# Moving eight first products of a lookup pass into the ranking stage, and six instead of two pairs behind the last expert weight

## The chip, the cores and the metric

The kernel runs on one core of a Trainium2 chip. The metric is the device time of one execution in microseconds (us). The core's engines are named as in the profile: PE multiplies matrices (PEld loads its weights), DVE works on vectors, ACT evaluates functions and also issues some DMAs, POOL is GpSimd, SP issues most DMAs.

## The reference

The program computes two blocks on 256 tokens of width 1024. The first is a token mixer with banded attention and a mixture of 32 experts (top 4). The second has two layers with a latent stream and a context stream of 256 tokens each. Each stream of a layer goes through a mixer and then through a large table lookup:

```python
def peer_ffn(h, w_q, sub_keys, u_tab, v_tab):
    # per block xb of 128 tokens
    q = (xb @ w_q).reshape(128, 8, 2, 64)
    s = einsum('thpd,pkd->thpk', q, sub_keys)       # 8 heads, 2 halves, 128 sub-keys
    s1, i1 = top_k(s[:, :, 0], 16); s2, i2 = top_k(s[:, :, 1], 16)
    cand_s = s1[..., :, None] + s2[..., None, :]    # 256 candidates
    cand_i = i1[..., :, None] * 128 + i2[..., None, :]
    top_s, pos = top_k(cand_s, 16)
    idx = take_along_axis(cand_i, pos); wts = softmax(top_s)
    act = gelu(einsum('thkd,td->thk', u_tab[idx], xb)) * wts
    return einsum('thk,thkd->td', act, v_tab[idx])  # tables of 16384 rows of 1024
```

The context stream goes through the first layer's lookup only. It depends on nothing of the first block, so its work can be done beside the experts.

## The kernel before

All 16384 rows of both tables are read and multiplied for all tokens (`peer_pass`, L838), in 64 pairs of 2 x 128 rows. The first product of a pair (`u_stage`, L861) is rows of `p_u` times the tokens; its gelu is the tile `ge`. `a_stage` (L898) multiplies it by a grid that is zero where a token did not choose a row and holds its weight where it did. The second product (`v_stage`, L921, `v_part` L908) multiplies the result by rows of `p_v` and adds it up in four PSUM banks of tag `a`. The product of a pair is done one pair after its first one.

Products of this kind are in three parts: `wload` (L141) loads 128x1024 weights (512 KB) into `wr`, ACT copies them rounded into `wh` (L147), DVE subtracts to get the rest `wl` (L148), and PE multiplies three times (L157 to L159 for the first product, L914, L915 and L917 for the second). `wr`, `wh` and `wl` have three buffers each.

`peer_prep` (L816) stands before a pass: queries (`p_w_q`), then `topk` (L719) for each of two blocks of 128 tokens, then `grid` (L787), which builds the selection grid and writes it to `gd` in DRAM. `topk` ranks on DVE; its last step takes the chosen table rows out of the candidates with one fused instruction for each head and place (L768), 128 for a block. `peer_pass` can do first products ahead of the pass (`ahead`): `early` pairs, whose `ge` is either kept or written to DRAM (`sdr`) and read back by `prefetch` (L886) some pairs ahead of its use. The two latent passes do 40 pairs so; the context pass none.

`moe` (L970) runs the experts two at a time: `expert_load` (L549) brings 24 weights of 1 MiB for such an expert pair into four buffers, all on SP's queue; gate and up products are L1096, the down product L1130, the scatter L1142 and its addition on DVE L1143. `overflow` (L1146) is a conditional block after the first two expert pairs.

The order of each engine's instructions is fixed ahead of time by a scheduler that goes by priorities and its own estimate of durations. Work inside `with filler()` has the lowest priority. There are two such stretches: the first holds the context mixer and the first eight steps (`PB`) of the context `peer_prep`; the second (L1267) holds the rest of it, and the context pass. Between them `overflow` and the remaining experts are written (`drain(mgen)`, L1266), with which the second stretch runs side by side. After them comes the latent branch (`chunk_mlp` with `a_w_v`, `a_w_u`, `a_w_out`, then its own `peer_prep` and pass).

`fetch` (L853) is the load of a pass. Where `late` is given, the loads of the last `late[0]` pairs are put behind the last expert weight in SP's order (`queued`):

```python
if late is not None and at_pair[0] >= npair - late[0]:
    queued(ins, late[1])
```

PSUM has eight banks: two of tag `g` (experts, latent products), two of `u`, four of `a`. In the kernel before, the context ranking takes `u` banks, the grid `a` banks and the context first products `u` banks.

## Time and profile before

| | us |
|---|---|
| median of 3 runs | 4162.1 |
| lowest, highest | 4159.7, 4166.0 |
| the profiled execution | 4160.3 |
| its span in the trace | 4158.5 |
| PE busy | 4020.3 (97%) |
| DVE busy | 2381.3 (57%) |
| ACT busy | 1929.3 (46%) |
| POOL busy | 169.7 (4%) |
| DMA | 1115 MB, mean 268 GB/s |

The span is what the trace shows; the time of the execution has 1.8 us more around it. Busy shares are means over stages that are limited by different things, so a stage is read by itself: which engine is full, what the granted clock of PE is (1.00 is 2.4 GHz, 0.50 is 1.2 GHz), and how much of DMA's time is used. Matmuls are pipelined: the mean duration of one is longer than the distance between two, and the distance is what it costs.

### The profile page before, as it was taken

The page shows a single profiled execution, that of the slowest core. Times are in us where ns is not written, and L with a number is a line of the kernel's source. Part 1 is how long each engine was busy: PE and PEld are TensorE (multiplying, and loading weights), DVE is VectorE, ACT ScalarE, POOL GpSimd, SP SyncE. Part 2 cuts the span into 40 slices and gives each one's busy share as a digit, 9 for nine tenths or more (in the row PEclk, how much of TensorE's full clock was granted, in tenths as well). Part 3 has the DMA queues.
Part 4 walks back from the last instruction along what each step waited for, and adds up shares of the span by engine and source line. Part 5 has one row for each costly group of instructions (what it writes and reads, how often), then busy time and mean ns, then how long its engine had stood idle before and what let it go on. Part 6 is the DMA issues. An engine that isn't in the chain of part 4 may idle for free.

```text
span 4158.5 us, 63267 instructions
## 1 busy us (share of the span) xinstructions
PE 4020.3 (97%) x23842; PEld 3070.1 (74%) x23842; DVE 2381.3 (57%) x6357; ACT 1929.3 (46%) x2836; POOL 169.7 (4%) x230
## 2 busy tenths in 40 slices
PE   8999979999999999999999999999998899999998
PEld 7676535566666666666588998788787699988887
DVE  4464696533333333333378996565455789766555
ACT  5543245433333333333243885345545349744443
POOL 0000001100000000000000120000000002200000
PEclk9999989999999999999999999999998899999999
DMA  7659879998889898998865679766774246787773
GB/s 255 243 189 360 326 285 345 363 337 321 340 325 341 318 344 310 352 344 323 314 198 171 211 257 327 255 227 220 259 255 146 97 153 232 261 289 242 236 236 126
DMA packets 340046, 1115.49 MB, mean 268 GB/s; under 512 B 28934, under 2 KB 128006, under 8 KB 283672
## 3 DMA queue, kind: packets, MB, share of 16 engines
q1 hardware_dynamic: 323896, 1043.22, 70.2%
q10 hardware_dynamic: 15552, 66.07, 4.0%
q8 instruction: 190, 3.11, 0.3%
q0 software_dynamic: 288, 2.10, 0.1%
q14 instruction: 120, 0.98, 0.1%
HBM read 1041.97 MB, written 69.30 MB: 267 GB/s over the span
## 4 chain that ended last, share of the span: by engine, by line
PE 74%; DVE 6%; DMA 4%; ACT 2%; issue 1%; SPq 0%; POOL 0%; ACTq 0%; DVEq 0%; POOLq 0%
PE ps_g L1096 9%; PE ps_a L915 8%; PE ps_a L914 8%; PE ps_a L917 8%; PE ps_u L157 8%; PE ps_u L158 8%; PE ps_u L159 8%; PE ps_g L1130 4%; PE ps_a L811 3%; PE ps_g L1142 1%; DVE wl L148 1%; DVE eq L768 1%; DMA mo<-in_w_up_dram 1%; DMA mo<-in_w_gate_dram 1%; PE ps_g L210 1%; PE ps_g L351 1%
## 5 line engine op out<-in xcount | busy, mean ns | idle before, releaser
L148 DVE TENSOR_TENSOR wl<-wr,wh 128x1024 fp32r<-128x1024 f32 x933 | 1131.8, 1221 | 1038.7 <-ACT wh L147 1031.7
L147 ACT ACTIVATE wh<-wr 128x1024 fp32r<-128x1024 f32 x933 | 979.5, 1055 | 1268.6 <-PE ps_u L158 523.4
L915 PE MATMUL ps_a<-wl,ah 128*128 128x512 f32 x1536 | 587.2, 398 | 3.3 <-DVE wl L148 3.1
L914 PE MATMUL ps_a<-wh,ah 128*128 128x512 f32 x1536 | 571.8, 397 | 1.1 <-ACT ah L117 1.1
L1096 PE MATMUL ps_g<-mo,xg 128*64 128x512 f32 x2048 | 471.5, 603 | 11.7 <-DMA mo<-in_w_up_dram 9.3
L917 PE MATMUL ps_a<-wh,al 128*128 128x512 f32 x1536 | 478.3, 396 | 0.2 <-DVE al L118 0.2
L914 PEld LDWEIGHTS ps_a<-wh,ah 128*128 128x128 f32 x1536 | 287.9, 188 | 80.3 <-issue 12.5
L915 PEld LDWEIGHTS ps_a<-wl,ah 128*128 128x128 f32 x1536 | 286.2, 188 | 76.8 <-issue 13.3
L917 PEld LDWEIGHTS ps_a<-wh,al 128*128 128x128 f32 x1536 | 286.7, 188 | 71.8 <-issue 6.1
L1096 PEld LDWEIGHTS ps_g<-mo,xg 128*64 128x64 f32 x2048 | 137.6, 137 | 264.4 <-issue 236.3
L157 PE MATMUL ps_u<-xbh,wh 128*128 128x256 f32 x1088 | 313.3, 288 | 0.0
L158 PE MATMUL ps_u<-xbl,wh 128*128 128x256 f32 x1088 | 312.7, 288 | 0.0
L159 PE MATMUL ps_u<-xbh,wl 128*128 128x256 f32 x1088 | 312.6, 287 | 0.0
L157 PE MATMUL ps_u<-xah,wh 128*128 128x256 f32 x960 | 275.9, 288 | 2.7 <-ACT sp L881 2.7
L159 PE MATMUL ps_u<-xch,wl 128*128 128x256 f32 x960 | 274.1, 287 | 4.4 <-DVE wl L148 4.4
L159 PE MATMUL ps_u<-xah,wl 128*128 128x256 f32 x960 | 273.8, 287 | 3.2 <-DVE wl L148 3.2
L158 PE MATMUL ps_u<-xal,wh 128*128 128x256 f32 x960 | 275.5, 287 | 0.0
L157 PE MATMUL ps_u<-xch,wh 128*128 128x256 f32 x960 | 274.5, 286 | 0.2 <-ACT wh L147 0.2
L158 PE MATMUL ps_u<-xcl,wh 128*128 128x256 f32 x960 | 274.5, 286 | 0.0
L810 DVE TENSOR_SCALAR o<-cst,it 128x128 f32<-128x128 f32 x768 | 231.9, 345 | 36.6 <-PE ps_a L811 36.1
L1130 PE MATMUL ps_g<-mo,hT 128*64 128x512 f32 x1024 | 238.9, 609 | 7.9 <-DMA mo<-in_w_down_dram 5.1
L811 PE MATMUL ps_a<-o,o 128*128 128x128 f32 x1536 | 227.3, 278 | 12.3 <-ACT o L806 9.3
(654 smaller groups left out, 7020.3 us busy)
## 6 DMA issues: line engine op xcount, KB each, us to landing
wr<-in_p_u_dram SPq DMA_DIRECT2D x384, 512.0 KB, 5.0
wr<-in_p_v_dram SPq DMA_DIRECT2D x384, 512.0 KB, 4.9
mo<-in_w_gate_dram SPq DMA_DIRECT2D x128, 1024.0 KB, 7.7
mo<-in_w_up_dram SPq DMA_DIRECT2D x128, 1024.0 KB, 6.9
mo<-in_w_down_dram SPq DMA_DIRECT2D x128, 1024.0 KB, 7.5
gd<-stg ACTq DMA_DIRECT2D x48, 1024.0 KB, 7.0
gr<-gd SPq DMA_DIRECT2D x96, 512.0 KB, 8.5
mw<-in_w_mod_dram SPq DMA_DIRECT2D x48, 512.0 KB, 4.3
```

The source lines that it names most:

```text
L147: nc.scalar.activation(wh[:, :n], wr[:, :n], AF.Copy)
L148: low = nc.vector.tensor_sub(wl[:, :n], wr[:, :n], wh[:, :n].bitcast(F32))
L157: nc.tensor.matmul(o, wh, xh, start=first, stop=False)
L158: nc.tensor.matmul(o, wh, xl, start=False, stop=False)
L159: nc.tensor.matmul(o, wl, xh, start=False, stop=last)
L810: nc.vector.tensor_scalar(o1, iota, it[:, 0, t:t + 1], it[:, 2, t:t + 1], op0=ALU.is_equal, op1=ALU.mult)
L811: nc.tensor.matmul(bank[:, 2 * i2 + i, :], o2q[:, i, :], o1, start=True, stop=True)
L914: nc.tensor.matmul(acc[tb][hf], ah[:, ts], wh[:, hs], start=first, stop=False)
L915: nc.tensor.matmul(acc[tb][hf], ah[:, ts], wl[:, hs], start=False, stop=False)
L917: last_mm[0] = nc.tensor.matmul(acc[tb][hf], al[:, ts], wh[:, hf * 512:(hf + 1) * 512], start=False, stop=fin).ins
L1096: nc.tensor.matmul(bank[64 * i:64 * i + 64, :], xg[:, kq * 4 + k, o:o + CAP], wt[i][:, k, :], start=(kq == 0 and k == 0), stop=False, skip ...
L1130: nc.tensor.matmul(bank[64 * i:64 * i + 64, :], hT[:, kq * 4 + k, 64 * i:64 * i + 64], wt[i][:, k, :], start=(kq == 0 and k == 0), stop=(k ...
```

## The change

- `peer_prep` of the context ranks in `a` banks instead of `u` banks (`"a"`), and its grid has four buffers of `o1` instead of six.
- The context pass is created before the conditional block. While `peer_prep` goes on, `bsteps` takes one early pair after every second step, eight in all (`N_AHEAD_B`): four are written ahead of the conditional block. Their first product is computed, gelu is applied, and the 128x512 result goes to DRAM through one buffer (`sp`). Their subtraction (L148) is done by GpSimd instead of DVE. In the pass, these results are read back into the two `ge` buffers (`pf=0`: in the pair's own step).
- The loads of the last six pairs (before: two) stand behind the last expert weight.
- In `topk`, for all three rankings, the fused instructions are replaced: for each of 16 places one comparison, one multiplication and one sum over 128x400, on one buffer.

```diff
--- before.py
+++ after.py
@@ -36,7 +36,8 @@
 QS = 4
 GB = 4
 GG = ('g','u','a','a')
-B_LATE = 2
+B_LATE = 6
+N_AHEAD_B = 8
 MT = "u"
 M1, M2, M3 = (2,4,8)
 MI = 14
@@ -138,15 +139,15 @@
     def load(dst, src):
         last_load[0] = nc.sync.dma_start(dst, src).ins
 
-    def wload(src, n=1024, get=load, s=None):
+    def wload(src, n=1024, get=load, s=None, eng=None):
         wr = wraw(s)
         get(wr[:, :n], src)
         pl, nb = s or (st, WB)
         wh = pl.tile([P, 1024], F32R, tag="wh", name="wh", bufs=nb[1])
         wl = pl.tile([P, 1024], F32R, tag="wl", name="wl", bufs=nb[1])
         nc.scalar.activation(wh[:, :n], wr[:, :n], AF.Copy)
-        low = nc.vector.tensor_sub(wl[:, :n], wr[:, :n], wh[:, :n].bitcast(F32))
-        if hold[1]:
+        low = (eng or nc.vector).tensor_sub(wl[:, :n], wr[:, :n], wh[:, :n].bitcast(F32))
+        if hold[1] and eng is None:
             queued(low, hold[0])
             hold[1] -= 1
         return wh, wl
@@ -762,12 +763,13 @@
             nc.vector.tensor_copy(tf, tx)
             ef = tk.tile([P, 8, 16], F32, tag="ef", name="ef")
             eqs = tk.tile([P, 8, 64], F32, tag="sc", name="eq", bufs=2)
-            for h in range(8):
-                for k in range(16):
-                    eq = eqs[:, k % 8, 0:NCAND]
-                    nc.vector.scalar_tensor_tensor(eq, iota[:, 0:NCAND], tf[:, h, k:k + 1], ce[:, h, :], op0=ALU.is_equal,
-                                                   op1=ALU.mult, accum_out=ef[:, h, k:k + 1])
-                if h % 2:
+            eq = eqs[:, :, 0:NCAND]
+            for k in range(16):
+                nc.vector.tensor_tensor(eq, iota[:, None, 0:NCAND].to_broadcast([P, 8, NCAND]), tf[:, :, k:k + 1].to_broadcast([P, 8, NCAND]),
+                                        op=ALU.is_equal)
+                nc.vector.tensor_mul(eq, eq, ce)
+                nc.vector.tensor_reduce(ef[:, :, k:k + 1], eq, axis=AX.X, op=ALU.add)
+                if k % 4 == 3:
                     yield
             ei = tk.tile([P, P], I32, tag="ts", name="ei")
             e2 = tk.tile([P, P], I32, tag="tx", name="e2")
@@ -835,7 +837,7 @@
         drain(first)
         yield from grid(tk, idx[1], gd[1], bufs, 2)
 
-    def peer_pass(l, xm, pp, gd, consume, ahead=None, after=None, late=None, mark=None, npair=64, wide_end=False):
+    def peer_pass(l, xm, pp, gd, consume, ahead=None, after=None, late=None, mark=None, npair=64, wide_end=False, sub_eng=None, pf=PF):
         xh, xl = v3(xm[0]), v3(xm[1])
         acc = []
         n_keep, n_nat, n_ahead, lead, span, ra, rs, xf = ahead or (0, 0, 0, 0, 1, None, None, None)
@@ -854,7 +856,7 @@
             ins = nc.sync.dma_start(dst, src)
             queued(ins, after[0] if after else None)
             if late is not None and at_pair[0] >= npair - late[0]:
-                queued(ins, late[1])
+                queued(ins, late[1]["last"])
             if mark is not None:
                 mark[:] = [ins.ins]
 
@@ -867,7 +869,7 @@
                     for k in range(KD):
                         nc.tensor.matmul(bank[:, c * T:(c + 1) * T], wr[:, k * P:(k + 1) * P], v3(xf)[:, k, :], start=(k == 0), stop=(k == KD - 1))
                 else:
-                    wh, wl = wload(a["p_u"][l, 2 * pr + c], get=load if pr in rank else fetch)
+                    wh, wl = wload(a["p_u"][l, 2 * pr + c], get=load if pr in rank else fetch, eng=sub_eng if pr in rank else None)
                     for k in range(KD):
                         s = slice(k * P, (k + 1) * P)
                         mm3(bank[:, c * T:(c + 1) * T], (wh[:, s], wl[:, s]), (xh[:, k, :], xl[:, k, :]), k == 0, k == KD - 1)
@@ -945,11 +947,13 @@
             if rank[pr] < n_keep:
                 kept[pr] = ge
             yield "ahead"
+        for p in range(pf):
+            prefetch(p)
         grid_fetch(0)
         prev = None
         for pr in range(npair):
             at_pair[0] = pr
-            prefetch(pr + PF)
+            prefetch(pr + pf)
             if pr % 4 == GP:
                 grid_fetch(pr // 4 + 1)
             ge = kept.pop(pr) if pr in rank else u_stage(pr, False)
@@ -963,6 +967,14 @@
             for hf in range(2):
                 consume(tb, hf, acc[tb][hf])
         yield npair
+
+    class Lent:
+        def __init__(self, pl, **bufs):
+            self.pl, self.bufs, self.alias = pl, bufs, {}
+
+        def tile(self, shape, dt, tag, name, bufs):
+            tag = self.alias.get(tag, tag)
+            return self.pl.tile(shape, dt, tag=tag, name=name, bufs=self.bufs.get(tag, bufs))
 
     gds = [[dr.tile([P, 8, P, 16], F32, name=f"gd{i}{b}") for b in range(2)] for i in range(3)]
 
@@ -1259,7 +1271,19 @@
         cx_stack.close()
         tkb_stack = ctx.enter_context(ExitStack())
         tkb = pool("tkb", stack=tkb_stack, side="right")
-        bprep = peer_prep(0, XB, tkb, gds[0], (2, NB1, 3), "u")
+        bpp, bsp = Lent(None), Lent(tkb, sp=1)
+        bpass = peer_pass(0, XB, bpp, gds[0], late_res(bres, cdr, 0, 1, 5, bpp, "gr"), late=(B_LATE, mres), mark=bmark,
+                          ahead=(0, 0, N_AHEAD_B, N_AHEAD_B, 1, None, bsp, None), sub_eng=nc.gpsimd, pf=0)
+        left = [N_AHEAD_B]
+
+        def bsteps():
+            for i, _ in enumerate(peer_prep(0, XB, tkb, gds[0], (2, 4, 3), "a")):
+                if i % 2 and left[0]:
+                    drain(bpass, 1)
+                    left[0] -= 1
+                yield
+
+        bprep = bsteps()
         drain(bprep, PB)
     overflow(mo, mres)
     general("g")
@@ -1267,10 +1291,12 @@
     with filler():
         general("u", "a")
         drain(bprep)
+        drain(bpass, left[0])
         tkb_stack.close()
         pp_stack = ctx.enter_context(ExitStack())
         pp = pool("pp", stack=pp_stack, side="right")
-        bpass = peer_pass(0, XB, pp, gds[0], late_res(bres, cdr, 0, 1, 5, pp, "gr"), late=(B_LATE, mres["last"]), mark=bmark)
+        bpp.pl = bsp.pl = pp
+        bsp.bufs, bsp.alias = {"ge": 2}, {"sp": "ge"}
         drain(bpass)
         general("g")
     acc = mres["acc"]
```

## Rows read from the trace of the kernel before

**Rows 1.** busy table by stage: PE, PEld, DVE, ACT, POOL (instructions), PEclk, DMA share, GB/s

```profile
...
500.00:650.00 150.00, 121.52 (x571) 58.31 (x570) 138.63 (x1037) 65.96 (x146) 14.05 (x22) 0.89 0.73 282
650.00:787.00 137.00, 128.43 (x766) 78.35 (x766) 77.19 (x263) 83.96 (x166) 30.50 (x42) 1.00 0.93 355
787.00:936.00 149.00, 147.01 (x795) 93.94 (x792) 55.43 (x71) 50.77 (x61) 0.00 (x0) 1.00 0.93 347
936.00:1872.00 936.00, 935.50 (x5099) 606.42 (x5098) 353.69 (x446) 326.10 (x390) 0.00 (x0) 1.00 0.89 333
...
2024.00:2090.00 66.00, 60.46 (x297) 33.17 (x296) 21.37 (x31) 17.31 (x22) 0.57 (x1) 0.97 0.73 279
...
2111.00:2220.00 109.00, 97.87 (x566) 85.67 (x566) 82.95 (x111) 43.68 (x53) 8.77 (x7) 0.92 0.59 193
2220.00:2520.00 300.00, 292.93 (x2367) 286.75 (x2366) 270.44 (x1346) 214.95 (x380) 48.51 (x64) 1.00 0.65 223
```

**Rows 2.** chain of waits: start, length in us, engine, tile, line, instructions

```profile
...
2043.61 3.58 PE ps_g L1096 x16
...
2088.10 0.47 PE ps_a L917 x2
...
2275.37 0.24 PE ps_u L159 x2
```

**Rows 3.** groups by line, PE, 936 to 1872 (busy, mean ns; idle before)

```profile
...
L1096 PE MATMUL ps_g<-mo,xg 128*64 128x512 f32 x1024 | 233.4, 598 | 0.5 <-DMA mo<-in_w_gate_dram 0.4
L157 PE MATMUL ps_u<-xbh,wh 128*128 128x256 f32 x720 | 207.6, 288 | 0.0
...
L915 PE MATMUL ps_a<-wl,ah 128*128 128x512 f32 x359 | 142.4, 402 | 0.0
...
L1130 PE MATMUL ps_g<-mo,hT 128*64 128x512 f32 x528 | 120.6, 598 | 0.0
```

**Rows 4.** groups by line, PE, 495 to 640

```profile
...
L1096 PE MATMUL ps_g<-mo,xg 128*64 128x512 f32 x150 | 37.4, 642 | 6.3 <-DMA mo<-in_w_up_dram 5.5 <-DMA mo<-in_w_gate_dram 0.8
...
L1142 PE MATMUL ps_g<-yo,pt 128*128 128x512 f32 x16 | 10.6, 760 | 7.9 <-DVE xst L1143 7.5 <-ACT pt L1138 0.5
```

**Rows 5.** timeline of SP's DMA issues, 300 to 700: start, length, line, load, count

```profile
...
470.18 0.33 SPq L854 DMA_DIRECT2D wr<-in_p_u_dram  x1
...
498.88 7.31 SPq L551 DMA_DIRECT2D mo<-in_w_down_dram  x4
533.14 2.76 SPq L551 DMA_DIRECT2D mo<-in_w_gate_dram  x4
...
619.43 6.37 SPq L551 DMA_DIRECT2D mo<-in_w_gate_dram  x4
```

**Rows 6.** groups by line, PE, 640 to 690

```profile
...
L157 PE MATMUL ps_u<-xbh,wh 128*128 128x256 f32 x32 | 9.4, 295 | 0.0
```

**Rows 7.** groups by line, DVE, 520 to 832

```profile
...
L148 DVE TENSOR_TENSOR wl<-wr,wh 128x1024 fp32r<-128x1024 f32 x11 | 13.4, 1223 | 21.1 <-ACT wh L147 21.0
...
L1108 DVE TENSOR_TENSOR gt<-gt,sg 128x512 f32<-128x512 f32 x6 | 4.1, 686 | 1.4 <-ACT sg L1105 1.4
```

**Rows 8.** one line, L800 on POOL: ns min/median/max, first and last start

```profile
...
L800 POOL TENSOR_SCALAR o<-cst,it x192: 595/660/2247, 559.7 to 3621.0; 128x128 f32<-128x128 f32 x192
```

**Rows 9.** chain of waits, 600 to 640

```profile
...
618.86 3.50 DVE eq L768 x36
```

**Rows 10.** timeline of SP's DMA issues, 1990 to 2300

```profile
...
2024.20 0.33 SPq L854 DMA_DIRECT2D wr<-in_p_v_dram  x1
...
2047.22 18.47 SPq L551 DMA_DIRECT2D mo<-in_w_down_dram  x8
...
2084.60 10.87 SPq L854 DMA_DIRECT2D wr<-in_p_v_dram  x4
2098.11 6.91 SPq L139 DMA_DIRECT2D wr<-in_a_w_v_dram  x3
```

**Rows 11.** busy table of 10 us, columns as in Rows 1

```profile
...
2050.00:2060.00 10.00, 8.86 (x41) 3.02 (x39) 1.39 (x2) 0.60 (x1) 0.00 (x0) 1.00 0.87 347
```

## The prediction

> **What bounds the kernel now.** I read the busy table by stage first. Times are us from the start of the span. In the long mixed stage, 936 to 1872, where expert weights and context lookup pairs run side by side, PE is busy 935.5 of 936 us at full clock, while the DMA share is 0.89 [rows 1]. A busy PE need not be a full one, so I looked at the chain's pieces: first-product matmuls follow each other every 0.12 us, second-product ones every 0.235 us, and sixteen expert matmuls take 3.58 us [rows 2]. The counts of that stage [rows 3] at those prices fill it: 2160 first-product matmuls (45 pairs; L157 is one of three equal lines) cost 259 us, 1077 second-product ones 253 us, and the expert matmuls of eight expert pairs (1024 and 528) 348 us; the small expert work (gathers, transposes, scatters) is the rest. So that stage is PE-bound. One context pair costs 48 x 0.12 = 5.8 us for its first product and 24 x 0.235 = 5.6 us for its second, 11.4 in all. An expert pair costs about 52 us of PE; with 5.6 context pairs it takes 117 us.
>
> The stage ahead of it is another case. From 500 to 650, while the context keys are ranked, PE is idle 28.5 of 150 us at a mean granted clock of 0.89 of the 2.4 GHz level, the DMA share is 0.73 and DVE is busy 138.6 us [rows 1]. PE waits there for expert weights and for DVE's additions, which stand in DVE's queue among ranking instructions [rows 4]; no first product runs there. The DMA queue has nothing to issue between the last loads at 498.88 to 506 and 533.14, where the conditional block ends [rows 5]. From 650 to 787 (selection grids) PE is idle 8.6 us at a DMA share of 0.93.
>
> From this follows how I count. Ahead of the latent branch (about 2100) the order of work is fixed and PE's work is nearly the same before and after. The time changes by what PE's unused time changes.
>
> **The first products that come early.** Eight pairs are 8 x 5.8 = 46 us of PE work, and 16 loads of 512 KB. In the kernel before, the weights of the first pairs are already loaded from 470.18 to 496 (four p_u, two p_v, the first of them in [rows 5]) and then sit in the buffers: the two pairs' matmuls run only at 640 to 690 [rows 6], when the ranking has given up the u banks. The change gives the ranking the a banks and so frees the u banks. Net new ahead of the pass are six pairs, 34.6 us. Room: 28.5 us idle in 500 to 650 and 8.6 us in 650 to 787, 37 together; the lost clock of the first stretch ((1 - 0.89) x 121.5 = 13 us) may come back in part. DMA: 8 MiB of p_u less the 3 MiB already early, plus 2 MiB of spilled results, is 7.3 MB; at 347/0.93 = 373 GB/s that is 20 us, against 0.27 x 150 = 40 us free. SP is moved past too: these loads stand among the expert loads and each waits for one of three buffers, with expert loads queued behind it. The ends are 0 (every block delays the experts by its length) and 37 + 13 = 50, of which at most 46 can be used; I take **24 us gained**, two thirds of the idle time, because a 5.8 us block put into gaps of 2 us displaces expert work that partly meets a DMA wait later.
>
> GpSimd's subtraction of 128x1024 is not in the trace. Nearest rows: the same operation on DVE, 1.22 us [rows 7], and a 128x128 GpSimd instruction, at least 0.595 us, times eight, 4.8 us [rows 8]. Sixteen cost 20 to 77 us in a stretch of 170, two of them beside 5.8 us of PE work for each pair; I count them as hidden, and at the upper end the pairs come at 9.6 us each, 77 us, which still fits. If nothing hid them, the early products would wait for them and the gain of 24 would be lost. The Trainium skill ("GPSIMD Engine Reference", Elementwise — side-by-side cycle accounting) measures 4497 ns for a two-input add of 2048; half, 2.25 us, would be an estimate from that page, 36 us for sixteen, and the sum would be the same.
>
> **The ranking's gather.** 128 fused instructions plus accumulator reads become 48 over 128x400. Now a pair takes 3.50/18 = 0.194 us [rows 9], 24.9 us per token block. A 128x512 two-input operation takes 0.686 and a 128x1024 one 1.223 [rows 7], so 400 elements give 0.686 - 112 x 0.00105 = 0.57 us; 48 in dependence are 27.4 us. If other instructions overlap their ends by some 0.09 us, 23 us. Six blocks change by -2 to +2.5 us each. In the latent rankings PE stays covered by early first products (292.9 of 300 us busy from 2220 to 2520, DVE 270.4 [rows 1]): **0**, ends -8 and +10 for both. In the context ranking DVE is the pace: about 5 us there, and some 8 us of blocking by GpSimd; at 19% unused PE that is **2 us lost**. The o1 buffers fall from six to four; the grid stage is DMA-heavy (0.93), so I count nothing, up to 5 us.
>
> **The first eight pairs of the pass** now bring 5.6 us of PE work per 1.5 MiB (p_v, grid, spilled result) instead of 11.4 per 2.25 MiB. Expert weights bring 52/24 = 2.2 us per MiB, a v-only pair 3.7, DMA takes 2.8. Mixed as now (a third context bytes) that is 2.7 against 2.8: DMA-bound by a little over some 33 MiB. The stage 787 to 936 already stands at 0.93 [rows 1]. **3 us lost**, ends 0 and 10.
>
> **The late pairs.** Six pairs behind the last expert weight mean 26 loads there instead of 10 (p_v runs one pair behind). Context work that must finish alongside the experts falls by 34.6 + 4 x 11.4 = 80 us. In the mixed stage context work takes 65 of 117 us, so its loads run out 80/0.55 = 145 us earlier; now they run out at 2024 with about 13 MiB of expert weights to issue [rows 10]. That leaves 13 + 1.24 x 24 = 43 MiB, less some 2 that the longer stretch before has taken: 41 MiB, 1.7 expert pairs. DMA: 43 MB/373 = 115 us. PE: 1.7 x 52 = 88 us plus the lag of context work that is loaded but not multiplied (now PE is full until its first idle after 2050, 26 us after 2024 [rows 11]): 114. So they balance, and waits break it: the present tail, 2024 to 2090, has 5.5 us idle [rows 1]; I take 12.5, **7 us lost**. Ends: -3, and +26 if experts alone go as slowly as at 533 to 619, 86 us per expert pair [rows 5]. The 26 late loads keep PE busy some 74 us and cover the latent chain's normalization and transposes as ten do now.
>
> **Sum:** -24 + 2 + 0 + 3 + 7 = -12 us. The profiled run took 4160.3 us (span 4158.5, 1.8 around it), 1.8 below the median 4162.1: 4148 for that run, **4150 us** for a median.
>
> **Rivals.**
> *Late pairs fill the latent gaps.* From 2111 to 2220 PE is idle 11 us at a clock of 0.92 [rows 1], 19 us of capacity. Four more pairs could fill 15: 4135. Against it: a_w_v loads need only a buffer, yet the first is issued at 2098.11, after the last late p_v of 2084.60 to 2095 [rows 10]; buffers of one kind seem given in program order, so late pairs finish ahead of the latent weights.
> *Slower: experts alone at the end.* With context work gone, PE meets only the experts' own chain (weights, activation, transposes, down product). At 86 us per expert pair the term is +26 instead of +7: 4169. It decides from 82 us on (1.7 x 82 - 114 - 5.5 = 19, what the other terms give). For it: the only stretch with experts alone shows 86. Against it: DVE was full of ranking there, and is idle at the end.
> *Two-input instructions block each other.* The trace has one sign: GpSimd's L800 takes 0.66 us at the median and once 2.247 [rows 8], while DVE runs many two-input operations. If a GpSimd subtraction holds DVE's two-input gather for its whole length, 16 of 1.2 to 4.8 us (20 to 77 us, geometric middle 39) lengthen a DVE-bound stretch that leaves 19% of PE unused: 7 us, 4157. The Trainium skill states such a rule ("SBUF — State Buffer", Who interferes with whom): the two engines share a port pair as an exclusive lock, taken by a DVE instruction with two SBUF inputs against a GpSimd one that reads SBUF, and the later fully blocks. L800's long case agrees with it; the mean of L148, 1.223 us, shows nothing of it, but no long GpSimd operation runs there.
> *It doesn't do what it says.* The static order sets most early products behind the ranking, into 650 to 787 with 8.6 us idle: a gain of 6 instead of 24, 4168.
>
> **How the numbers follow.** Chances: forecast 0.42, latent gaps 0.13, experts alone 0.20, blocking 0.15, not early 0.10. A measurement of this kernel can tell about 0.2%, 8.3 us, from no change. Faster: 0.36 of the forecast, all of the gaps, 0.03 of blocking: 0.52. Slower: 0.14 of experts alone, 0.04 of not early, 0.03 of blocking: 0.21. Within: 0.27. The range: early gain 24 (10 to 40), tail +7 (-3 to +26) and the latent gaps give 4130 to 4173.
>
> **What would show it.** First products (L157, xb) between 490 and 650, with PE idle there falling from 28 to about 10 us and the conditional block no later than some 533 to 540; the pass starting 5 to 15 us later than 793; the last expert weight issued some 65 to 85 us earlier than 2065 with DMA at about 0.95 ahead of it; 26 p_u and p_v loads behind it; the first a_w_v load about 10 us earlier than 2098. Wrong would be: the ranking stretch longer by over 20 us, expert pairs alone above 80 us with PE idle over 20 us in the tail, or first products that still begin near 640. An a_w_v load earlier than the last late p_v would speak for filled gaps.

## The result and the profile after

The change made the kernel slower: 4212.3 us (median; 4208.9 to 4217.4) against 4160.9 for the kernel before, ratio 1.0123 [1.0111, 1.0136], about +51 us. The prediction was 4150 us within 4130 to 4173, so sign and range were both wrong. Lines stand lower in the kernel after, by one near its start and by twelve past `peer_pass`: L148 is L149, L157 is L158, the grid's product L811 is L813, and the expert products L1096 and L1130 are L1108 and L1142.

The busy table of the kernel after, by stage (PE, PEld, DVE, ACT, POOL with instructions, granted PE clock, DMA share, GB/s), to be held against [rows 1]:

```profile
...
500.00:650.00 150.00, 131.84 (x798) 85.20 (x796) 133.26 (x568) 72.24 (x126) 40.58 (x27) 0.94 0.77 287
650.00:787.00 137.00, 118.47 (x628) 64.16 (x625) 78.62 (x240) 77.31 (x168) 24.46 (x37) 0.98 0.89 322
787.00:936.00 149.00, 137.40 (x645) 77.52 (x645) 63.17 (x152) 50.74 (x76) 9.37 (x15) 0.98 0.96 358
936.00:1872.00 936.00, 936.00 (x5109) 606.70 (x5107) 356.17 (x448) 328.78 (x394) 0.00 (x0) 1.00 0.88 333
1872.00:2000.00 128.00, 121.55 (x618) 68.98 (x614) 35.02 (x46) 32.55 (x44) 0.00 (x0) 0.99 0.82 309
2000.00:2080.00 80.00, 57.69 (x230) 19.76 (x229) 10.95 (x14) 7.10 (x10) 0.00 (x0) 0.89 0.81 311
2080.00:2144.00 64.00, 64.00 (x410) 57.05 (x409) 45.89 (x64) 33.89 (x41) 2.07 (x2) 1.00 0.65 214
```

The stretches from 1872 to 2080 of the kernel before:

```profile
...
1872.00:2000.00 128.00, 128.00 (x702) 83.07 (x702) 46.20 (x56) 45.70 (x57) 0.00 (x0) 1.00 0.83 312
2000.00:2080.00 80.00, 74.46 (x368) 40.07 (x365) 22.83 (x29) 22.49 (x27) 0.00 (x0) 0.98 0.83 328
```

Part of the idle time that was to be filled is filled: from 500 to 650 PE idles 18.2 us instead of 28.5 (about 10 was expected). But it idles 18.5 instead of 8.6 in the grid stage, 11.6 instead of 2.0 from 787 to 936, and 28.8 instead of 5.5 from 1872 to 2080. SP's issues in the kernel after say the same:

```profile
...
519.18 25.79 SPq L140 DMA_DIRECT2D wr<-in_p_u_dram  x5
550.84 2.83 SPq L552 DMA_DIRECT2D mo<-in_w_gate_dram  x4
553.72 12.33 SPq L140 DMA_DIRECT2D wr<-in_p_u_dram  x3
...
847.00 0.63 SPq L856 DMA_DIRECT2D gr<-gd  x1
...
1933.99 0.33 SPq L856 DMA_DIRECT2D wr<-in_p_v_dram  x1
...
1967.80 17.61 SPq L552 DMA_DIRECT2D mo<-in_w_down_dram  x8
...
2042.89 24.23 SPq L552 DMA_DIRECT2D mo<-in_w_down_dram  x8
...
2132.42 8.92 SPq L856 DMA_DIRECT2D wr<-in_p_v_dram  x4
2143.76 15.19 SPq L140 DMA_DIRECT2D wr<-in_a_w_v_dram  x6
```

The conditional block ends at 550.8 (533.1 in [rows 5]); the pass starts with its first grid load at 847.0 (793.5 before); context loads run out at 1934 and two blocks of down-weights follow, 75 us apart, the last of them issued by 2067, no earlier than before; the first latent weight comes at 2143.8 instead of 2098.1 [rows 10]. From there to the end both kernels take the same: 2063 and 2060 us. So 46 us, nearly all of the difference, arise ahead of the latent branch.

### The profile page after: what moved, and what is told of

Same layout as the page of the kernel before. It is cut to its first block, busy times and chain, and to the rows that moved or that the text cites. A ratio compares the mean times of both kernels' runs of the same rounds, so it can differ in the third digit from the quotient of the medians.

```text
span 4207.1 us, 62082 instructions
## 1 busy us (share of the span) xinstructions
PE 4032.3 (96%) x23842; PEld 3075.1 (73%) x23842; DVE 2387.7 (57%) x5093; ACT 1925.4 (46%) x2833; POOL 211.0 (5%) x246
## 4 chain that ended last, share of the span: by engine, by line
PE 73%; DMA 5%; DVE 5%; ACT 2%; issue 1%; SPq 0%; POOL 0%; ACTq 0%; DVEq 0%; POOLq 0%
PE ps_g L1108 8%; PE ps_a L916 8%; PE ps_a L917 8%; PE ps_a L919 8%; PE ps_u L158 8%; PE ps_u L159 8%; PE ps_u L160 8%; PE ps_g L1142 5%; PE ps_a L813 3%; DMA mo<-in_w_up_dram 2%; PE ps_g L1154 1%; DMA mo<-in_w_down_dram 1%; DMA wr<-in_p_v_dram 1%; DMA mo<-in_w_gate_dram 1%; DVE wl L149 1%; PE ps_g L211 1%
## 5 line engine op out<-in xcount | busy, mean ns | idle before, releaser
L149 DVE TENSOR_TENSOR wl<-wr,wh 128x1024 fp32r<-128x1024 f32 (+1 forms) x917 | 1113.0, 1220 | 936.2 <-ACT wh L148 922.1
L148 ACT ACTIVATE wh<-wr 128x1024 fp32r<-128x1024 f32 x933 | 982.3, 1055 | 1229.3 <-PE ps_u L159 462.8
L1108 PE MATMUL ps_g<-mo,xg 128*64 128x512 f32 x2048 | 472.8, 605 | 25.2 <-DMA mo<-in_w_up_dram 16.1
L1108 PEld LDWEIGHTS ps_g<-mo,xg 128*64 128x64 f32 x2048 | 137.9, 138 | 282.3 <-issue 242.6
L158 PE MATMUL ps_u<-xbh,wh 128*128 128x256 f32 x1024 | 296.4, 289 | 3.1 <-DVEq L1163 3.1
L159 PE MATMUL ps_u<-xbl,wh 128*128 128x256 f32 x1024 | 295.5, 289 | 0.0
L160 PE MATMUL ps_u<-xbh,wl 128*128 128x256 f32 x1024 | 293.2, 286 | 0.0
L158 PE MATMUL ps_u<-xah,wh 128*128 128x256 f32 x960 | 275.0, 287 | 1.6 <-ACT sp L883 1.6
L158 PE MATMUL ps_u<-xch,wh 128*128 128x256 f32 x960 | 274.0, 285 | 1.3 <-ACT sp L883 1.3
L1142 PE MATMUL ps_g<-mo,hT 128*64 128x512 f32 x1024 | 245.2, 622 | 17.7 <-DMA mo<-in_w_down_dram 17.7
L813 PE MATMUL ps_a<-o,o 128*128 128x128 f32 x1536 | 227.2, 282 | 22.5 <-DVE o L812 11.4
```

What stands on the lines that cost most here:

```text
L148: nc.scalar.activation(wh[:, :n], wr[:, :n], AF.Copy)
L149: low = (eng or nc.vector).tensor_sub(wl[:, :n], wr[:, :n], wh[:, :n].bitcast(F32))
L158: nc.tensor.matmul(o, wh, xh, start=first, stop=False)
L159: nc.tensor.matmul(o, wh, xl, start=False, stop=False)
L160: nc.tensor.matmul(o, wl, xh, start=False, stop=last)
L813: nc.tensor.matmul(bank[:, 2 * i2 + i, :], o2q[:, i, :], o1, start=True, stop=True)
```

## The experiments

Times are medians; the ratio is to the kernel before, run in the same round, with its 95% interval; 0.001 is 4.2 us. A profile is one execution, and executions of one kernel lie 7 to 26 us apart, so prices are taken from ratios and places from traces. Kernels that start from the kernel before have its line numbers. Every edit also makes the scheduler place other work anew, so a step of a few us can't be told from such a shift.

### Each part of the change alone

**Six late pairs in the kernel before.**

```diff
-B_LATE = 2
+B_LATE = 6
```

> The kernel before with six late pairs and nothing else. Theory 1: context loads run out 45.6/0.55 = 82 us earlier, some 1.2 expert pairs go alone at 75 us each, PE idles 15 to 25 us more at the end: 4176 to 4186. Theory 2: within 5 us of the kernel before, 4156 to 4166.

4178.9 us, 1.0052 [1.0034, 1.0069]: +22 us. Its busy table in the tail, in steps of 20 us:

```profile
...
1980.00:2000.00 20.00, 15.98 (x56) 4.99 (x54) 4.14 (x6) 1.67 (x2) 0.00 (x0) 0.91 0.88 347
2000.00:2020.00 20.00, 14.07 (x58) 4.63 (x60) 2.77 (x4) 0.63 (x1) 0.00 (x0) 0.97 0.96 376
2020.00:2040.00 20.00, 15.03 (x66) 5.53 (x63) 1.38 (x2) 1.20 (x2) 0.00 (x0) 0.95 0.88 331
```

Once context loads have run out, PE is busy 45 of 60 us while DMA stands at 0.88 to 0.96. The last expert weights are issued 24 us earlier (2041 for 2065), but 26 instead of 10 loads then stand ahead of the first latent weight, which comes 22 us later (2120).

**The new gather in the kernel before.**

Shortened:

```diff
-   for h in range(8): for k in range(16): scalar_tensor_tensor(.., accum_out=ef[:, h, k:k + 1])
+   for k in range(16): tensor_tensor, tensor_mul, tensor_reduce over 128x400
```

> The kernel before with the ranking's gather in 48 instructions over 128x400 instead of 128 fused ones, in all three rankings. If 48 dependent instructions of 0.57 us and gaps of 0.03 make up 29 us for a block against 24.9, DVE has 4 us more for each of six blocks: covered by PE in the latent stages it costs 0 to 8 us in all (4161 to 4169), not covered 24 us (4185).

4169.5 us, 1.0021 [1.0007, 1.0034]: +8.7 us for six token blocks. The 48 instructions depend on each other and start every 0.61 us (568.60, 569.21, 569.82 in the DVE timeline below), 29 us for a block against the 24.9 counted from [rows 9].

**Four grid buffers instead of six.**

```diff
-peer_prep(0, XB, tkb, gds[0], (2, NB1, 3), "u")
+peer_prep(0, XB, tkb, gds[0], (2, 4, 3), "u")
```

> The kernel before with four o1 buffers instead of six in the context grid; nothing else. The grid stage stands at a DMA share of 0.93, so theory a gives no change (within 4 us) and a grid end within 5 us of 787. If DVE's lead over PE in the grid is what counts, the grid ends 10 to 30 us later and the time rises by 5 to 15 us.

4179.0 us, 1.0046 [1.0028, 1.0064]: +19 us, more than either theory; the pass starts at 854 instead of 793. DVE's groups by line from 680 to 790 (busy, mean ns, idle before and what ended it), first the kernel before, then this one:

```profile
...
L810 DVE TENSOR_SCALAR o<-cst,it 128x128 f32<-128x128 f32 x148 | 44.5, 353 | 28.8 <-PE ps_a L811 28.7
L802 DVE TENSOR_SCALAR o<-cst,it 128x128 f32<-128x128 f32 x64 | 15.5, 290 | 0.3 <-PE ps_a L811 0.3
```

```profile
...
L810 DVE TENSOR_SCALAR o<-cst,it 128x128 f32<-128x128 f32 x115 | 34.7, 351 | 41.9 <-PE ps_a L811 41.8
L802 DVE TENSOR_SCALAR o<-cst,it 128x128 f32<-128x128 f32 x34 | 8.2, 284 | 0.0
```

In the same 110 us DVE fills 149 grid buffers instead of 212, and waits 42 us for PE to read one. PE's fixed order has expert products between the grid's; I take it that, while PE works on those, DVE can write ahead into six buffers, but soon runs out of four.

**Ranking in the a banks, in the kernel before.**

```diff
-peer_prep(0, XB, tkb, gds[0], (2, NB1, 3), "u")
+peer_prep(0, XB, tkb, gds[0], (2, NB1, 3), "a")
```

> The kernel before with the context ranking in a banks, which the grid uses, instead of u banks; nothing else. In the early-only kernel the second token block's ranking ends at 672 to 683 but its indices are turned only at 721 (before: 643 and 654), and the pass starts 54 us late. Theory a (banks): the ranking waits for grid banks; the pass starts 15 to 35 us later than 793 and the time rises by 8 to 20 us. Theory b (the early products' own work on PE, DMA and GpSimd): no change, 4150 to 4163, pass start near 795.

4184.9 us, 1.0053 [1.0036, 1.0070]: +22 us. The tile `it` is the copy of a token block's indices out of PSUM, with which its grid begins; `ei` (L774) is the end of its ranking (ns min/median/max, first and last start). First the kernel before, then this one:

```profile
...
L783 ACT ACTIVATE it<-ps_u x2: 483/484/486, 559.1 to 654.1; 128x384 f32<-128x384 f32 x2
...
L774 DVE CAST ei<-ef x2: 226/226/227, 556.3 to 642.9; 128x128 int32<-128x128 f32 x2
```

```profile
...
L783 ACT ACTIVATE it<-ps_a x2: 471/480/490, 573.8 to 692.8; 128x384 f32<-128x384 f32 x2
...
L774 DVE CAST ei<-ef x2: 214/216/217, 563.2 to 658.9; 128x128 int32<-128x128 f32 x2
```

From the end of the second block's ranking to its indices are 11 us with u banks and 34 us with a banks: the transposes now stand among the products of the first block's grid, which uses the a banks. But the pass starts at 802, only 8 us late, where 15 to 35 were expected, and the time rises by more than the 8 to 20 of that theory. So the late indices are shown, and the price; that the one makes the other is not.

**Both together.**

```diff
-peer_prep(0, XB, tkb, gds[0], (2, NB1, 3), "u")
+peer_prep(0, XB, tkb, gds[0], (2, 4, 3), "a")
```

> The kernel before with a banks for the context ranking and four o1 buffers: what the change takes from the ranking and the grid to make room, without any early product. Theory s (the two prices stack and the early products do gain): 4190 to 4200, 13 to 23 us slower than the early-only kernel with DVE subtractions (4177). Theory n (both hold up the same grid, and early products gain nothing): 4177 to 4186, the same as that kernel.

4177.9 us, 1.0051 [1.0032, 1.0070]: +21 us. The two don't add up. Why is open: the pass starts at 854 with four buffers, at 802 with a banks and at 829 with both, so it isn't the later of two delays of one grid that counts, and the pass's start doesn't measure the price.

### From both together to the full change, one part at a time

**Early products, with DVE's subtraction** (two late pairs, the fused gather). Against the kernel just shown it differs only by the early products; against the next one, by this:

```diff
-sub_eng=nc.gpsimd, pf=0)
+sub_eng=None, pf=0)
```

> The early-only kernel with the sixteen early subtractions on DVE (1.22 us each) instead of GpSimd (2.4 us). If the two engines' blocking of each other lengthens the ranking, this is 5 to 20 us faster than the early-only kernel (4174 to 4189). If the GpSimd placement does what it is for, DVE gets 20 us more in its full stretch and this is 0 to 10 us slower.

4177.4 us, 1.0042 [1.0027, 1.0057]: by the ratios 4 us less than without them, with intervals that overlap. 46 us of PE work brought forward are worth next to nothing.

**The same with GpSimd's subtraction.** The edit is the kernel after with two late pairs and the fused gather.

> The changed kernel with two late pairs and the old gather: the eight early first products alone, with their banks, their GpSimd subtraction and four o1 buffers. Theory 1: the early part costs what the pass starts later without PE being fuller: 10 to 20 us, 4172 to 4182. If the gather makes the late start, it is 4150 to 4163, and the pass starts near 800 instead of 847. If the early part is what was meant, PE idle in 500 to 850 falls by over 15 us.

4193.8 us, 1.0093 [1.0074, 1.0112]: slower than any of the three theories, and +21 us for the engine alone, by ratios of two rounds; the two profiled executions, 4185.0 and 4182.3 us, are only 3 us apart. The busy table from 530 to 560, first with GpSimd, then with DVE, and the PE wait that only the first one has (L1153 is the experts' scatter, L1154 DVE's addition):

```profile
...
530.00:560.00 30.00, 16.27 (x87) 13.90 (x87) 29.62 (x215) 5.82 (x8) 7.10 (x3) 0.72 0.42 147
...
PE ps_g L1153 <- DVE xst L1154: 8.3, 1, 8.3
```

```profile
...
530.00:560.00 30.00, 24.48 (x171) 21.55 (x168) 28.98 (x207) 14.45 (x18) 0.00 (x0) 0.94 0.55 200
```

With GpSimd PE idles 13.7 of these 30 us, 8.3 of them for DVE's addition (the other 5.5, for the start of the conditional block, stand in both); with DVE's subtraction it has 130 first-product matmuls to do there, against 81, and doesn't wait for the addition. The kernel before has such a wait too, 7.5 us [rows 4]: with GpSimd it stays, with DVE's subtraction it is gone. How GpSimd and DVE meet is in the trace of the kernel after: first the sixteen subtractions (ns min/median/max, first and last start), then GpSimd's and DVE's timelines (start, length, line), last a one-input instruction of the ranking, in both blocks:

```profile
...
L149 POOL TENSOR_TENSOR wl<-wr,wh x16: 2344/2395/2802, 487.9 to 582.4; 128x1024 fp32r<-128x1024 f32 x16
```

```profile
...
527.34 2.42 POOL L149 TENSOR_TENSOR wl<-wr,wh 128x1024 fp32r<-128x1024 f32 x1 [1.33 <-ACT wh L148]
...
563.18 2.51 POOL L149 TENSOR_TENSOR wl<-wr,wh 128x1024 fp32r<-128x1024 f32 x1 [0.82 <-ACT wh L148]
569.20 2.80 POOL L149 TENSOR_TENSOR wl<-wr,wh 128x1024 fp32r<-128x1024 f32 x1 [3.51 <-ACT wh L148]
```

```profile
...
563.51 2.62 DVE L770 TENSOR_TENSOR eq<-eq,ce 128x400 f32<-128x400 f32 x1
...
568.60 0.58 DVE L768 TENSOR_TENSOR eq<-cst,tx 128x400 f32<-128x400 f32 x1
569.21 0.57 DVE L770 TENSOR_TENSOR eq<-eq,ce 128x400 f32<-128x400 f32 x1
569.82 0.57 DVE L771 TENSOR_REDUCE ef<-eq 128x8 f32<-128x400 f32 x1
570.42 2.02 DVE L768 TENSOR_TENSOR eq<-cst,tx 128x400 f32<-128x400 f32 x1
```

```profile
...
L741 DVE TENSOR_SCALAR x<-x x2: 207/1122/2037, 527.8 to 625.5; 128x128 f32<-128x128 f32 x2
```

L770, 0.58 us elsewhere, takes 2.62 and ends 0.44 us after GpSimd's instruction (563.18 + 2.51); L768 at 570.42 does the same behind the next one, while the one-input sum L771 at 569.82 runs through beside it. The Trainium skill ("SBUF — State Buffer", Who interferes with whom) states this as an exclusive lock: a DVE instruction with two SBUF inputs contends with a GpSimd one that reads SBUF, issue order decides which of them is blocked, and a `tensor_reduce` never contends on trn2. The trace agrees, 2.62 us against 0.57. It shows the other order too: L770 at 569.21 starts with a GpSimd subtraction and keeps its 0.57 us, and that subtraction takes 2.80 instead of 2.40. One input alone is no safeguard: L741 takes 2.04 us beside the subtraction of 527.34, and 0.21 where none runs.

In the gather of the kernel after, the lengthened instructions sum to 3.9 us (means of 0.702 and 0.694 us instead of 0.575, sixteen of each). But the 21 us belong to the pair of kernels with the fused gather, and there the lock costs more. DVE's groups from 485 to 585, with GpSimd's subtraction, then with DVE's:

```profile
...
L769 DVE SCALAR_TENSOR_TENSOR eq<-cst,tx,ce 128x50 f32<-128x50 f32 x128 | 38.0, 361 | 0.0
```

```profile
...
L769 DVE SCALAR_TENSOR_TENSOR eq<-cst,tx,ce 128x50 f32<-128x50 f32 x128 | 25.5, 266 | 0.0
L149 DVE TENSOR_TENSOR wl<-wr,wh 128x1024 fp32r<-128x1024 f32 x17 | 20.6, 1218 | 12.8 <-ACT wh L148 12.8
```

GpSimd spares DVE 20.6 us of subtractions there, and holds the gather of one block for 12.5 us more and three other instructions of the ranking (L741, L747, L749) for 5.3. So DVE is relieved of some 3 us, not of 20. In both pairs of kernels that differ by this engine (the second follows below) PE then idles 9 us more from 500 to 650 with GpSimd (20.6 against 11.6 us, and 21.4 against 12.2), 8.3 of them in the one wait for DVE's addition. How much of that wait is the lock and how much the other order that the scheduler writes isn't separated, and neither is the rest of the 21 us.

**Four early products instead of eight, GpSimd.**

```diff
-N_AHEAD_B = 8
+N_AHEAD_B = 4
```

> The early-only kernel with four early pairs instead of eight (all four are written ahead of the conditional block). If each early pair costs its share, half of the 38 us is left (4175). If only the banks cost, the time stays at 4185 to 4195. If the first four fill idle PE and the rest hurt, it comes to 4150 to 4165.

4168.9 us, 1.0025 [1.0015, 1.0035]: 28 us better than eight, between its share (4175) and the theory of idle time filled (4150 to 4165). The fused instructions (ns min/median/max) with eight, then with four:

```profile
...
L769 DVE SCALAR_TENSOR_TENSOR eq<-cst,tx,ce x256: 222/261/2425, 535.8 to 672.2; 128x50 f32<-128x50 f32 x128
```

```profile
...
L769 DVE SCALAR_TENSOR_TENSOR eq<-cst,tx,ce x256: 214/264/289, 535.9 to 659.4; 128x50 f32<-128x50 f32 x128
```

With four, GpSimd's last subtraction starts at 525.6, ahead of the gather, and no fused instruction is held; the longest wait for DVE's addition is 3.9 us instead of 8.3, though PE, with less to do, idles more from 500 to 650 (24.7 us for 20.6). The pass also starts with fewer pairs whose first product is gone (at 834 instead of 847); this run doesn't tell the two apart.

**All but the late pairs** (the kernel after with two).

```diff
-B_LATE = 6
+B_LATE = 2
```

> The changed kernel with two late pairs instead of six. Theory 1 (the late pairs leave the experts alone at the end, where PE runs dry): the idle time of PE ahead of the latent branch, 26 us in 1976 to 2080 of the changed kernel, falls to about 6, and the time to 4185 to 4192. Theory 2 (all is lost where the pass starts 54 us later, and the late pairs only take up what is left): the time stays within 8 us of 4212, since the work that no longer waits at the end is only done in another order.

4204.1 us, 1.0105 [1.0084, 1.0126]: 8 us less, the edge of the second theory, and far from the 4185 to 4192 of the first. So the ladder in ratios is: banks and grid buffers 1.0051, with early products 1.0042, with GpSimd 1.0093, with the gather 1.0105, with the late pairs 1.0123. In us: +21, -4, +21, +5, +8, together +51. The first and the third step stand clear of their intervals, the others don't. Six late pairs, +22 alone, bring only +8 here. I take it that with eight first products gone context work runs out beside the experts anyway: with two late pairs its last other load is issued at 2019, and the last expert weights from 2077 on.

### Where the early products' gain goes

**Six grid buffers given back.** The spilled results get a buffer elsewhere, and the grid its six buffers (otherwise the kernel with DVE's subtraction):

```diff
-bpp, bsp = Lent(None), Lent(tkb, sp=1)
+bpp, bsp = Lent(None), Lent(sm, rt=1)
+bsp.alias = {"sp": "rt"}
-peer_prep(0, XB, tkb, gds[0], (2, 4, 3), "a")
+peer_prep(0, XB, tkb, gds[0], (2, NB1, 3), "a")
```

> The early-only kernel with DVE subtractions and six o1 buffers (the spilled result goes through a buffer of another pool that is free at that time, so it fits). If the four o1 buffers hold up the grid here as they do alone, 12 to 20 us less than 4177: 4157 to 4165, pass start near 825. If the early pairs fill the time that the grid loses, no change.

4168.4 us, 1.0019 [1.0009, 1.0030]: 10 us better, with intervals that overlap a little.

**Banks given back too.** The early products use a banks, the ranking u banks (shortened):

```diff
-            bank = psum("u")
+            bank = psum("a" if pr in rank else "u")
-peer_prep(0, XB, tkb, gds[0], (2, NB1, 3), "a")
+peer_prep(0, XB, tkb, gds[0], (2, NB1, 3), "u")
```

> Early products with everything left in place: ranking in u banks as in the kernel before, six o1 buffers, subtractions on DVE, two late pairs, old gather; the eight early products take a banks. If the price of the change lies in banks, buffers and GpSimd, the fill of the ranking stage is left: 10 to 25 us faster than the kernel before (4133 to 4148). If early products themselves cost (their DMA ahead of expert weights, no first products left to cover the pass's start), it is 4155 to 4170.

4170.4 us, 1.0036 [1.0020, 1.0052]: no better. Here every cost found so far is taken away, and 46 us of early work still don't pay: this kernel is 15 us slower than the kernel before, clear of its interval.

**The same with GpSimd's subtraction.**

```diff
-sub_eng=None, pf=0
+sub_eng=nc.gpsimd, pf=0
```

> The same as y3 with the early subtractions on GpSimd. If GpSimd's 2.4 us subtractions and DVE's two-input instructions block each other for their length, 8 to 20 us slower than y3. If DVE's relief counts more, 3 to 10 us faster.

4186.2 us, 1.0064 [1.0045, 1.0084]: +12 us, with intervals that overlap; the direction of the 21 us above.

**What is left to cover the pass's start.** In the kernel before, pairs with first products run at 640 to 690 [rows 6] and again from 790 to 830 (26 to each of the three lines), beside the grid and beside expert weights still under way. In the kernel after, at 840 to 850:

```profile
...
840.00:850.00 10.00, 5.43 (x14) 1.92 (x16) 0.00 (x0) 0.00 (x0) 0.00 (x0) 0.68 1.00 392
```

PE's groups by line from 830 to 860 (busy, mean ns, idle before):

```profile
...
L1142 PE MATMUL ps_g<-mo,hT 128*64 128x512 f32 x64 | 17.5, 697 | 5.5 <-DMA mo<-in_w_down_dram 5.5
L1154 PE MATMUL ps_g<-yo,pt 128*128 128x512 f32 x8 | 4.2, 632 | 1.2 <-ACT yo L1145 0.7 <-ACT pt L1150 0.5
L813 PE MATMUL ps_a<-o,o 128*128 128x128 f32 x12 | 2.1, 297 | 0.1
```

No context product is among them: the first eight pairs have only second products, which need the grid, and its first load is issued at 847. So I spread the eight early pairs (every fourth of the first 32) in the kernel with banks, buffers and subtraction given back:

```diff
-ahead=(0, 0, N_AHEAD_B, N_AHEAD_B, 1, None, bsp, None)
+ahead=(0, 0, N_AHEAD_B, 0, 32, None, bsp, None)
```

> The kernel of y3_swap (early products in a banks, the ranking in u banks, six grid buffers, DVE's subtraction, two late pairs, fused gather), but every fourth pair of the first 32 is early instead of the first eight. Theory: with the ranking's idle time filled and every cover kept, the gain was lost because the first eight pairs of the pass have no first product left to cover the pass's start, where PE was nearly empty between 830 and 860. Then the spread pairs keep that start full: PE idle in 787 to 936 falls from 8.6 us in y3_swap to 3 or less, and the time falls by 6 to 15 us, to between 4153 and 4164, at or below the kernel before. Rival: the loss lies elsewhere (the grid stage, experts alone at the end since early pairs took away context work); then the idle time at the start may fall but the tail takes it, and the time stays at 4168 to 4178.

4159.8 us, 1.0006 [0.9994, 1.0018]: level with the kernel before and 12 us (0.0030) better than the first eight, with intervals that just don't meet. So which pairs are early decides over some 12 of the 15 us. PE's idle time from 787 to 936 falls from 8.6 to 4.6 us, not quite to the 3 that were expected, and in the grid stage ahead of it from 18.7 to 14.2. Then where is the rest? Its busy table:

```profile
...
787.00:936.00 149.00, 144.44 (x771) 89.57 (x772) 69.24 (x166) 65.06 (x93) 10.86 (x17) 1.00 0.96 360
...
2000.00:2080.00 80.00, 60.96 (x232) 20.09 (x232) 8.29 (x12) 5.31 (x8) 0.00 (x0) 0.92 0.87 337
2080.00:2144.00 64.00, 63.52 (x331) 49.89 (x328) 50.00 (x70) 34.01 (x41) 2.58 (x3) 0.99 0.64 212
```

The tail has 19.0 us idle, against 5.5 before. So I gave it two more pairs beside the experts:

```diff
-B_LATE = 2
+B_LATE = 0
```

> The kernel of z1_spread with no late pairs instead of two. In z1_spread the context loads run out near 1972 and PE is idle 19 us from 2000 to 2080, against 5.5 in the kernel before, since the early products took context work away from the experts; this would be the 12 to 15 us that the early products gain and lose again. Theory: two more pairs beside the experts cut that idle time to 8 to 14 us and give 3 to 10 us, 4150 to 4157. Rival: the late pairs are then missing under the latent chain's start (2080 to 2144), where idle time grows by as much; the time stays at 4158 to 4166, as one late pair in the kernel before did.

4163.0 us, 1.0013 [1.0004, 1.0023]: the rival. The idle time moves by one stretch:

```profile
...
2000.00:2080.00 80.00, 74.00 (x347) 38.77 (x345) 24.83 (x33) 17.95 (x22) 0.00 (x0) 0.96 0.84 321
2080.00:2144.00 64.00, 49.82 (x204) 30.81 (x205) 31.70 (x48) 19.34 (x26) 1.45 (x2) 0.89 0.54 192
```

6.0 us idle beside the last experts and 14.2 under the latent chain's start, which the late pairs had covered. And eight grid buffers in the spread kernel:

```diff
-NB1 = 6
+NB1 = 8
```

> The kernel of z1_spread with eight grid buffers instead of six. Eight gave the kernel before some 5 us. If the grid stage of z1_spread (650 to 787, PE idle 14 us) waits for a free buffer, eight give 3 to 10 us here too: 4150 to 4157, with PE idle there at 10 or less and the pass starting before 838. If it waits for DVE or DMA (share 0.91), no change: 4157 to 4162, and the idle time of the tail stays near 19 us.

4158.1 us, 0.9995 [0.9985, 1.0005]: no change that can be told; the grid stage idles 12.2 instead of 14.2 us, the tail 16.3 from 2000 to 2080.

PE's idle time in us, from the busy tables of one execution each, shows where it went:

| stretch | before | after | first eight, all given back | spread | spread, none late |
|---|---|---|---|---|---|
| 416 to 500 | 2.6 | 3.5 | 3.4 | 3.9 | 4.6 |
| 500 to 650 | 28.5 | 18.2 | 12.2 | 11.9 | 12.1 |
| 650 to 787 | 8.6 | 18.5 | 18.7 | 14.2 | 13.0 |
| 787 to 936 | 2.0 | 11.6 | 8.6 | 4.6 | 4.4 |
| 936 to 1872 | 0.5 | 0.0 | 1.6 | 0.0 | 0.0 |
| 1872 to 2000 | 0.0 | 6.5 | 0.0 | 0.0 | 0.0 |
| 2000 to 2080 | 5.5 | 22.3 | 9.5 | 19.0 | 6.0 |
| 2080 to 2144 | 0.0 | 0.0 | 2.9 | 0.5 | 14.2 |
| sum | 47.7 | 80.6 | 56.9 | 54.1 | 54.3 |

Some 16 us are gained in the ranking in each of the last three, and each time given back elsewhere. The sums don't rank the kernels: the execution of the third column took 4157.1 us, the fastest of eight and 13 us below their median, and 3 us less than that of the kernel before, which idles 9 us less; behind the first latent weight it took 2046 us against 2060.

### Two sizes of the kernel before

**Eight grid buffers.**

```diff
-NB1 = 6
+NB1 = 8
```

> The kernel before with eight grid buffers of o1 instead of six, and nothing else. Six instead of four were worth 19 us. If the grid stage still waits for a free buffer at six, eight give 3 to 15 us more: 4145 to 4157, with the pass starting before 790. If six were enough, no change within 0.2%. The scheduler places work by these buffers, so a shift of the order either way, up to 15 us slower, is the third case.

4154.0 us against 4158.3, 0.9987 [0.9977, 0.9997]: 5 us faster, the only version that beats the kernel before clear of its interval, by less than the 0.2% that I call a difference. The pass starts at 780 instead of 793.

**One late pair.**

```diff
-B_LATE = 2
+B_LATE = 1
```

> The kernel before with one late pair instead of two, and nothing else. Six instead of two cost 22 us, because the experts ended without context work beside them. If the same holds at two, one late pair gives 2 to 8 us: 4152 to 4158, the first latent weight issued some 8 us earlier than 2098. If two are needed to cover the latent chain's normalization and transposes, it is 3 to 8 us slower, with PE idle after 2110 higher by about that.

4164.3 us, 1.0009 [0.9998, 1.0020]: no gain. PE's idle time moves as it did with none: 0.0 us from 2000 to 2080, 8.0 from 2080 to 2144. The late pairs' cost is not linear: two are near the best, and six cost 22 us.

## Why the prediction was wrong

**What held.** The mixed stage is PE-bound (936.00 of 936 us busy after). The early loads come where I put them, the first at 473 and the last by 566, and fill part of the ranking's idle time; that they would come too late is refuted. 26 loads stand behind the last expert weight, and the first latent weight waits for all of them (2132.42, then 2143.76), as I argued against the rival of filled gaps.

**Which steps failed.** By the ladder the forecast's -12 and the measured +51 lie 63 us apart: 17 in the early products (-24 and +3 against -4), 21 in the ranking's banks and the grid's buffers (nothing against +21), 21 in GpSimd's subtraction (nothing against +21), 3 in the gather and 1 in the late pairs.

**The term of -24 us.** It took 24 us off for idle time filled, and then priced what was left behind with 3 us. But first products are work that needs no grid, and there were only a few such pairs between 640 and 860; taken away, they uncover the grid stage and the pass's start. Measured: -4 us with the change's banks and buffers, +15 with all of these given back, and no gain even where the early pairs are spread over the pass. "The time changes by what PE's unused time changes" was the rule; I applied it to the stretch that receives the work and not to those that give it. Of what I listed as its signs, the conditional block was to end by 533 to 540 and ended at 551, the pass was to start 5 to 15 us late and started 54 us late, and the last expert weight was to come 65 to 85 us earlier and didn't. Of its mark for being wrong in the tail, PE's idle time over 20 us came (22.3 from 2000 to 2080), the 80 us for an expert pair alone did not (75).

**The edits that I counted at nothing** cost most. For the grid buffers I wrote "nothing, up to 5"; they cost 19 alone. The a banks I used only as what frees the u banks, and gave the ranking's move no price at all: 22 alone, 21 with the grid buffers. For the buffers a row stood ready: the grid's groups of lines in the kernel before show DVE waiting 28.8 us for PE to free one, and I read the DMA share of that stage instead.

**The tail.** I had +7 with +26 as the upper end; alone it is +22. The balance of 115 us of DMA against 114 of PE took both to run without a break. Alone, an expert pair takes 75 us (1967.80 to 2042.89), more than its 52 us of PE and than the 67 us of its 24 MiB at my 2.8 us. PE's waits from 1990 to 2080 are for expert weights, 20.2 us; that they come in order through four buffers may be why, but no run varied it. The rival "experts alone at the end" had the mechanism; its 86 us, taken from a stretch full of ranking, was too slow. Its point of decision, 82 us, was wrong because the other terms didn't give the 19 us that it set against it.

**GpSimd.** I counted its sixteen subtractions as hidden, with 7 us in the rival of blocking. Their length was right (2.40 us at the median, 38 us for sixteen, within 20 to 77). They cost 21 and 12 us in two pairs of kernels. I took GpSimd as free relief for DVE; the rival of blocking had the mechanism, and where the gather is fused the holds take back 17.8 of the 20.6 us that DVE is spared. The Trainium skill's estimate from "GPSIMD Engine Reference" (Elementwise — side-by-side cycle accounting), 2.25 us for one, stands 6% under the measured 2.40. The sum by it would have been the same.

**The gather.** 29 us a block instead of the 23 to 27.4 that I worked out: no overlap of their ends, but a gap of 0.03 us between them. With six blocks +8.7 us alone, where I had 2 for the context's blocks and 0 for the latent ones, with +10 as their end. I may have taken the latent rankings' cover too much for whole, with DVE busy 270 of 300 us there [rows 1]; no run tells the blocks apart.

**What stays open.** Some 12 of the 21 us of GpSimd, beyond the 9 that PE idles more in the ranking. Where the 22 us of the ranking's move to a banks arise, and why the prices of banks, buffers and late pairs don't add. The early results also cross DMA twice, 4.1 MB more in all (1119.6 for 1115.5), 11 us at my 373 GB/s, and are read back in the pair's own step; no run kept them on the chip or read them earlier, so this isn't separated from the lost cover. Of the 46 us by which the first latent weight is late, 33 are idle time of PE by the table; the other 13 (clock, among it 0.89 from 2000 to 2080, and late pairs' work ahead of it) I didn't take apart.

## What to carry to other kernels

When work that needs nothing is moved into a gap, price the place it comes from as carefully as the gap: ask which stretch had only that work to run, and look there for a transfer or a buffer that then ends last. Buffers and banks that are "merely" renamed or cut are terms of the sum; for buffers the groups of lines show already who waits for them, and alone they can cost as much as the whole gain. In a kernel like this one, with PE and DMA both near full, spread such work rather than take the first of it, and expect that the gain can be lost again at the end, where one of the two runs out of partner. Work that is moved to an idle engine is free only if it doesn't hold the busy one.

## What the runs showed of the hardware

A two-input DVE instruction of 0.58 us took 2.62 us beside a GpSimd subtraction and ended 0.44 us after it, while a one-input sum ran through beside the same kind of instruction in 0.57. The holds lengthened 128 fused DVE instructions from 25.5 to 38.0 us. A one-input `TENSOR_SCALAR` of 0.21 us took 2.04 beside such a subtraction. A 128x1024 subtraction takes GpSimd 2.40 us and DVE 1.22 [rows 7]. Dependent DVE instructions of 0.575 us start every 0.61 us. PE's granted clock, 0.99 of its 2.4 GHz level from 1872 to 2000, was 0.89 in the next 80 us, in which PE worked 57.69 us in pieces between weights, and 1.00 in the stretch behind them, where it was busy 64.00 of 64 us.
